# A streaming average pool: the last 14 of 64 row blocks loaded in pieces that step down in size, the small sizes in buffers of their own

## The chip, the cores and the metric

The kernel runs on one core of a Trainium2 chip. The metric is the device time of one execution in microseconds (us). All executions below are of the undisturbed ("fast") state, at a granted clock of 1.0. The span of the profile is 1.8 us shorter than that time (343.0 against 344.8 us in the profiled run of the kernel before).

Three engines matter. The DMA engines bring the input in and take the output out. VectorE (DVE in the profile) sums. ScalarE (ACT) multiplies by 1/16 and issues stores. SyncE (SP) only issues loads, and GpSimd (POOL) is idle before the change. A DMA that has landed raises a counter, its completion semaphore, and whoever needs its data waits for that counter. L75 in a view is line 75 of the kernel.

## The reference

```python
batch, channels, length = 32, 256, 4096      # float32, 134 MB
output_size = 256
for i in range(output_size):
    start = int(i * length / output_size)    # always 16 columns
    end = int((i + 1) * length / output_size)
    result[:, :, i] = np.mean(x[:, :, start:end], axis=-1)
```

The input is 8192 rows of 4096 numbers, 64 row blocks of 128 rows (2 MB each). Each block gives a 128 x 256 output (128 KB).

## The kernel before

The rows stream through. 31 pieces are pairs of blocks (4 MB, each partition one run of 32 KB), then there is one block of 2 MB, then the last block in four quarters of 512 KB. All 36 pieces rotate through the same four 32 KB-per-partition buffers.

```python
RBULK, IN_BUFS, TAIL_BLOCKS, TAIL_SPLITS = 2, 4, 2, 4       # (read from the environment; cut)
# pieces: (first block, blocks, first column, columns); pairs, one single, four quarters
# ... (cut)
sbuf = ctx.enter_context(tc.tile_pool(name="sbuf", bufs=IN_BUFS))
spool = ctx.enter_context(tc.tile_pool(name="spool", bufs=3))
opool = ctx.enter_context(tc.tile_pool(name="opool", bufs=3))

for (rb, nrb, c0, ncols) in pieces:
    # ... xin, oin: views of input and output (cut)
    xt = sbuf.tile([P, RBULK, length], x.dtype, name="xt")
    st = spool.tile([P, RBULK, length // k], mybir.dt.float32, name="st")
    ot = opool.tile([P, RBULK, length // k], out.dtype, name="ot")
    xv = xt[:, :nrb, :ncols]
    nc.sync.dma_start(out=xv, in_=xin)
    sv = st[:, :nrb, :nout]
    nc.vector.reduce_sum(out=sv, in_=xv.rearrange("p r (o k) -> p r o k", k=k),
                         axis=mybir.AxisListType.X)
    ov = ot[:, :nrb, :nout]
    nc.scalar.mul(out=ov, in_=sv, mul=inv_k)
    nc.scalar.dma_start(out=oin, in_=ov)
```

## Time and profile before

| | before |
|---|---|
| time, median of the first 5 runs | 344.8 us (344.77 to 345.09) |
| span | 343.0 us |
| bytes moved | 134.2 MB read, 8.4 MB written |
| VectorE busy | 278.2 us, 81% |
| DMA share and rate, 40 to 320 us | 1.00 to 1.01, 430 to 433 GB/s |

The first view is the table of windows of the kernel before. Its columns are the stretch, its length, the busy time of VectorE, ScalarE and GpSimd (with the number of instructions), the clock, the mean busy share of the 16 DMA engines, and GB/s. A packet's bytes and its time are counted in the stretch in which it starts, so a share can pass 1.

```profile
280.00:320.00 40.00, 34.25 (x4) 1.89 (x3) 0.00 (x0) 1.00 1.01 433
320.00:325.00 5.00, 3.35 (x2) 0.63 (x1) 0.00 (x0) 1.00 0.93 394
325.00:330.00 5.00, 5.00 (x1) 0.00 (x0) 0.00 (x0) 1.00 0.87 356
330.00:335.00 5.00, 5.00 (x2) 0.63 (x1) 0.00 (x0) 1.00 0.54 156
335.00:340.00 5.00, 4.38 (x5) 1.19 (x4) 0.00 (x0) 1.00 0.48 146
340.00:343.00 3.00, 0.38 (x1) 0.26 (x1) 0.00 (x0) 1.00 0.10 22
```

From 40 to 320 us the DMA engines are full. The Trainium skill ("DMA: Bandwidth & Descriptors", section "Where 436 GB/s comes from") puts the ceiling of the 16 ports at 435.2 GB/s; the 430 to 433 GB/s of this trace agree. From 320 us on the DMA share falls, to 0.54 in 330 to 335 us, while VectorE works without a break from 322.1 to 338.5 us. The last 23 us moved about 5.3 MB, 12.3 us of work at 432 GB/s, so some 10.7 us are lost here.

The second view is the end of the chain that ended last: start, duration, and what it was.

```profile
311.81 8.70 DVE st L75
...
320.52 9.79 DMA xt<-in_x_dram
...
330.74 4.42 DVE st L75
...
335.18 3.89 DMA xt<-in_x_dram
...
339.16 1.23 DVE st L75
...
340.41 0.26 ACT ot L81
```

Two of the quarters stand in this chain as loads, and each starts as a reduce ends: the second at 320.52, when the reduce of a pair gave up a buffer, and the fourth at 335.18, when the reduce of the 2 MB block did.

The third view is the groups of instructions by shape: line, engine, operation, output and input, count, busy time, mean of one in ns, and idle time before them.

```profile
L75 DVE TENSOR_REDUCE st<-xt 128x512 f32<-128x8192 f32 x31 | 269.3, 8686 | 61.6 <-DMA xt<-in_x_dram 61.6
L75 DVE TENSOR_REDUCE st<-xt 128x64 f32<-128x1024 f32 x4 | 4.7, 1213 | 0.6 <-DMA xt<-in_x_dram 0.6
L75 DVE TENSOR_REDUCE st<-xt 128x256 f32<-128x4096 f32 x1 | 4.4, 4409 | 0.0
```

A pair takes VectorE 8.69 us and arrives every 10.3 us. VectorE is therefore less than 20% faster than the stream.

### The profile page before, as it was taken

What the parts mean: (1) busy time and instruction counts of PE and PEld (TensorE: products, weight loads), DVE (VectorE), ACT (ScalarE), POOL (GpSimd) and SP (SyncE); (2) the same over time, 40 slices, a digit from 0 to 9 for tenths busy, and PEclk for the clock granted to TensorE, in tenths of its full rate; (3) what the DMA queues carried; (4) which work ended last, traced back from release to release, by engine and by line L of the source; (5) the groups of instructions that cost most, each with busy time, mean ns of one, the idle gap of its engine ahead of it and who ended that gap; (6) DMA issues with size and microseconds to landing.
All of it is one profiled execution on the core that took longest, in us unless ns stands there. A gap on an engine that the chain in (4) does not pass through costs nothing.

```text
span 343.0 us, 294 instructions
## 1 busy us (share of the span) xinstructions
DVE 278.2 (81%) x36; ACT 22.2 (6%) x37; POOL 0.2 (0%) x4
## 2 busy tenths in 40 slices
DVE  0488898888898888998888988888988888988896
ACT  1000000000000000000000000000000000000001
POOL 0000000000000000000000000000000000000000
DMA  8999999999999999999999999999999999999963
GB/s 321 447 436 413 451 427 418 451 412 440 447 406 442 447 401 455 430 411 455 427 421 451 409 436 451 406 447 431 410 454 431 413 458 411 430 451 415 425 239 107
DMA packets 10370, 142.63 MB, mean 416 GB/s; under 512 B 1664, under 2 KB 1792, under 8 KB 6272
## 3 DMA queue, kind: packets, MB, share of 16 engines
q1 hardware_dynamic: 5184, 134.22, 91.3%
q10 hardware_dynamic: 5184, 8.39, 6.4%
q14 instruction: 2, 0.02, 0.0%
HBM read 134.22 MB, written 8.39 MB: 416 GB/s over the span
## 4 chain that ended last, share of the span: by engine, by line
DMA 77%; DVE 22%; issue 0%; SPq 0%; ACT 0%; DVEq 0%
DMA xt<-in_x_dram 77%; DVE st L75 22%; SPq L73 0%; ACT ot L81 0%; DVEq L75 0%
## 5 line engine op out<-in xcount | busy, mean ns | idle before, releaser
L75 DVE TENSOR_REDUCE st<-xt 128x512 f32<-128x8192 f32 (+2 forms) x36 | 278.2, 7737 | 62.2 <-DMA xt<-in_x_dram 62.2
L81 ACT ACTIVATE ot<-st 128x512 f32<-128x512 f32 (+2 forms) x36 | 20.9, 582 | 317.7 <-DVE st L75 315.9
L81 ACT ACT_TABLE_LOAD x1 | 1.3, 1283 | 0.7 <-PEq L99 0.7
L99 POOL MEMSET const-uint8-127<- 128x1 uint8 x1 | 0.1, 103 | 0.0
L99 POOL MEMSET const-bfloat16-1.0<- 128x1 bf16 x1 | 0.1, 102 | 0.0
L99 POOL MEMSET const-float32-0.0<- 128x1 f32 x1 | 0.1, 99 | 0.2 <-issue 0.2
L99 POOL MEMSET const-float32-1.0<- 128x1 f32 x1 | 0.1, 99 | 0.0
## 6 DMA issues: line engine op xcount, KB each, us to landing
xt<-in_x_dram SPq DMA_DIRECT2D x31, 4096.0 KB, 32.5
out_dram<-ot ACTq DMA_DIRECT2D x31, 256.0 KB, 14.8
xt<-in_x_dram SPq DMA_DIRECT2D x1, 2048.0 KB, 27.6
xt<-in_x_dram SPq DMA_DIRECT2D x4, 512.0 KB, 6.9
out_dram<-ot ACTq DMA_DIRECT2D x1, 128.0 KB, 3.8
out_dram<-ot ACTq DMA_DIRECT2D x4, 32.0 KB, 1.8
```

The source lines that it names most:

```text
L75: nc.vector.reduce_sum(out=sv, in_=xv.rearrange("p r (o k) -> p r o k", k=k), axis=mybir.AxisListType.X,)
L81: nc.scalar.mul(out=ov, in_=sv, mul=inv_k)
L99: nc = _bacc.Bacc("TRN2", target_bir_lowering=False, num_devices=1)
```

## The change

The intent is to keep the DMA engines full to the last byte and to leave little work after it. The last 14 blocks are no longer pairs: ten are loaded as 2 MB pieces (still in the four big buffers), two in halves (1 MB), one in quarters (512 KB) and one in eighths (256 KB). Each of the three small sizes has as many buffers as its loads, so these 16 loads wait for no reduce to free a buffer. (Five of them still wait for the store of an earlier block, whose completion semaphore they take over: 17.8 us in all by SyncE's waits after.) The outputs of the blocks in halves and quarters are stored whole by GpSimd, that of the last block by ScalarE.

```diff
-    IN_BUFS = 4; TAIL_BLOCKS = 2; TAIL_SPLITS = 4          (from the environment; shortened)
+    # (shortened; the pools of sums and outputs are cut)
+    A_BUFS = 4; N1 = 10; NH = 2; NQ = 1; NE = 1; C_BUFS = 4; D_BUFS = 4
+    pa = tile_pool(bufs=A_BUFS)    # pairs and the ten single blocks
+    pc = tile_pool(bufs=C_BUFS)    # halves
+    pd = tile_pool(bufs=D_BUFS)    # quarters
+    pe = tile_pool(bufs=8)         # eighths
 ... (pairs as before; then N1 times the same with one block)
+    def tail_block(row0, splits, pool, tile_cols, last=False):
+        ob = ot.tile([P, output_size], f32, name="ob")
+        for (c0, ncols) in splits:
+            ...
+            xt = pool.tile([P, tile_cols], x.dtype, name="xc")
+            sv = st.tile([P, tile_cols // k], f32, name="sc")
+            xv = xt[:, :ncols]
+            nc.sync.dma_start(out=xv, in_=in_view(row0, 1, c0, ncols)[:, 0, :])
+            nc.vector.reduce_sum(out=sv[:, :nout], in_=xv.rearrange(...), ...)
+            nc.scalar.mul(out=ob[:, o0 : o0 + nout], in_=sv[:, :nout], mul=inv_k)
+        (nc.scalar if last else nc.gpsimd).dma_start(out=out_view(row0, 1, 0, output_size)[:, 0, :], in_=ob)
+    for _ in range(NH): tail_block(row0, [(0, half), (half, half)], pc, half)
+    for _ in range(NQ): tail_block(row0, [(i * quar, quar) for i in range(4)], pd, quar)
+    for _ in range(NE): tail_block(row0, [(i * eigh, eigh) for i in range(8)], pe, eigh, last=True)
```

More of the change, by code (lines that the diff above doesn't have):

```diff
@@ L33 @@
     n_blocks = n_rows // P
+    f32 = mybir.dt.float32
     RBULK = int(os.environ.get("AAP_RBULK", "2"))
-    IN_BUFS = int(os.environ.get("AAP_IN_BUFS", "4"))
-    TAIL_BLOCKS = int(os.environ.get("AAP_TAIL_BLOCKS", "2"))
-    TAIL_SPLITS = int(os.environ.get("AAP_TAIL_SPLITS", "4"))
-    pieces = []
-    nb_bulk = n_blocks - TAIL_BLOCKS
-    b = 0
-    while b < nb_bulk:
-        r = min(RBULK, nb_bulk - b)
-        pieces.append((b, r, 0, length))
-        b += r
-    while b < n_blocks - 1:
-        pieces.append((b, 1, 0, length))
-        b += 1
@@ L50 @@
-    if b < n_blocks:
-        assert length % (TAIL_SPLITS * k) == 0
-        c = length // TAIL_SPLITS
-        for s in range(TAIL_SPLITS):
-            pieces.append((b, 1, s * c, c))
-    sbuf = ctx.enter_context(tc.tile_pool(name="sbuf", bufs=IN_BUFS))
-    spool = ctx.enter_context(tc.tile_pool(name="spool", bufs=3))
-    opool = ctx.enter_context(tc.tile_pool(name="opool", bufs=3))
-    for (rb, nrb, c0, ncols) in pieces:
-        nout = ncols // k
-        row0 = rb * P
-        xin = x_flat[row0 : row0 + nrb * P, c0 : c0 + ncols]
-        xin = xin.rearrange("(p r) l -> p r l", r=nrb)
-        oin = out_flat[row0 : row0 + nrb * P, c0 // k : c0 // k + nout]
-        oin = oin.rearrange("(p r) l -> p r l", r=nrb)
-        xt = sbuf.tile([P, RBULK, length], x.dtype, name="xt")
-        st = spool.tile([P, RBULK, length // k], mybir.dt.float32, name="st")
-        ot = opool.tile([P, RBULK, length // k], out.dtype, name="ot")
-        xv = xt[:, :nrb, :ncols]
-        nc.sync.dma_start(out=xv, in_=xin)
-        sv = st[:, :nrb, :nout]
+    A_BUFS = int(os.environ.get("AAP_A_BUFS", "4"))
@@ new lines @@
+    N1 = int(os.environ.get("AAP_N1", "10"))
+    NH = int(os.environ.get("AAP_NH", "2"))
+    NQ = int(os.environ.get("AAP_NQ", "1"))
+    NE = int(os.environ.get("AAP_NE", "1"))
+    C_BUFS = int(os.environ.get("AAP_C_BUFS", "4"))
+    D_BUFS = int(os.environ.get("AAP_D_BUFS", "4"))
+    tail_blocks = N1 + NH + NQ + NE
+    nb_bulk = n_blocks - tail_blocks
+    assert nb_bulk >= 0 and nb_bulk % RBULK == 0
+    pa = ctx.enter_context(tc.tile_pool(name="pa", bufs=A_BUFS))
+    pc = ctx.enter_context(tc.tile_pool(name="pc", bufs=C_BUFS))
@@ new lines, with in_view @@
+    pd = ctx.enter_context(tc.tile_pool(name="pd", bufs=D_BUFS))
+    pe = ctx.enter_context(tc.tile_pool(name="pe", bufs=8))
+    sa = ctx.enter_context(tc.tile_pool(name="sa", bufs=2))
+    oa = ctx.enter_context(tc.tile_pool(name="oa", bufs=3))
+    st = ctx.enter_context(tc.tile_pool(name="st", bufs=4))
+    ot = ctx.enter_context(tc.tile_pool(name="ot", bufs=3))
+    half = length // 2
+    quar = length // 4
+    eigh = length // 8
+    def in_view(row0, nrb, c0, ncols):
+        v = x_flat[row0 : row0 + nrb * P, c0 : c0 + ncols]
+        return v.rearrange("(p r) l -> p r l", r=nrb)
@@ new lines, in out_view @@
+    def out_view(row0, nrb, o0, nout):
+        v = out_flat[row0 : row0 + nrb * P, o0 : o0 + nout]
+        return v.rearrange("(p r) l -> p r l", r=nrb)
+    blk = 0
+    while blk < nb_bulk:
+        nrb = RBULK
+        row0 = blk * P
+        xt = pa.tile([P, RBULK, length], x.dtype, name="xt")
+        sv = sa.tile([P, RBULK, output_size], f32, name="sv")
+        ov = oa.tile([P, RBULK, output_size], out.dtype, name="ov")
+        xv = xt[:, :nrb, :]
+        nc.sync.dma_start(out=xv, in_=in_view(row0, nrb, 0, length))
@@ L75 @@
         nc.vector.reduce_sum(
-            out=sv,
+            out=sv[:, :nrb, :],
             in_=xv.rearrange("p r (o k) -> p r o k", k=k),
@@ L79 @@
         )
-        ov = ot[:, :nrb, :nout]
-        nc.scalar.mul(out=ov, in_=sv, mul=inv_k)
-        nc.scalar.dma_start(out=oin, in_=ov)
+        nc.scalar.mul(out=ov[:, :nrb, :], in_=sv[:, :nrb, :], mul=inv_k)
+        nc.scalar.dma_start(out=out_view(row0, nrb, 0, output_size), in_=ov[:, :nrb, :])
+        blk += nrb
+    for _ in range(N1):
+        row0 = blk * P
+        xt = pa.tile([P, RBULK, length], x.dtype, name="xt")
+        sv = sa.tile([P, RBULK, output_size], f32, name="sv")
+        ov = oa.tile([P, RBULK, output_size], out.dtype, name="ov")
+        xv = xt[:, :1, :]
+        nc.sync.dma_start(out=xv, in_=in_view(row0, 1, 0, length))
+        nc.vector.reduce_sum(
+            out=sv[:, :1, :],
+            in_=xv.rearrange("p r (o k) -> p r o k", k=k),
+            axis=mybir.AxisListType.X,
+        )
+        nc.scalar.mul(out=ov[:, :1, :], in_=sv[:, :1, :], mul=inv_k)
+        nc.scalar.dma_start(out=out_view(row0, 1, 0, output_size), in_=ov[:, :1, :])
+        blk += 1
+    def tail_block(row0, splits, pool, tile_cols, last=False):
+        ob = ot.tile([P, output_size], f32, name="ob")
+        for (c0, ncols) in splits:
+            nout = ncols // k
+            o0 = c0 // k
+            xt = pool.tile([P, tile_cols], x.dtype, name="xc")
+            sv = st.tile([P, tile_cols // k], f32, name="sc")
+            xv = xt[:, :ncols]
+            nc.sync.dma_start(out=xv, in_=in_view(row0, 1, c0, ncols)[:, 0, :])
+            nc.vector.reduce_sum(
+                out=sv[:, :nout],
+                in_=xv.rearrange("p (o k) -> p o k", k=k),
+                axis=mybir.AxisListType.X,
+            )
+            nc.scalar.mul(out=ob[:, o0 : o0 + nout], in_=sv[:, :nout], mul=inv_k)
+        (nc.scalar if last else nc.gpsimd).dma_start(out=out_view(row0, 1, 0, output_size)[:, 0, :], in_=ob)
+    for _ in range(NH):
+        row0 = blk * P
+        tail_block(row0, [(0, half), (half, half)], pc, half)
+        blk += 1
+    for _ in range(NQ):
+        row0 = blk * P
+        tail_block(row0, [(i * quar, quar) for i in range(4)], pd, quar)
+        blk += 1
+    for _ in range(NE):
+        row0 = blk * P
+        tail_block(row0, [(i * eigh, eigh) for i in range(8)], pe, eigh, last=True)
+        blk += 1
+    assert blk == n_blocks
 _INS = ['x', 'output_size']
```

## The prediction

> **What bounds it now.** The input stream. In the windows view the DMA share is 1.00 to 1.01 and 430 to 433 GB/s in every 40 us stretch from 40 to 320 us; the Trainium skill ("DMA: Bandwidth & Descriptors", "Where 436 GB/s comes from") gives a ceiling of 435.2 GB/s, and this trace agrees. DVE is not the limit there: a bulk reduce takes 8.69 us (groups by form) against 10.3 us between pieces (timeline: reduces start at 280.85, 291.16, 301.49, 311.81) and waits 1.6 us for data each time.
>
> Only the ends are not full. Start: the first reduce begins at 13.06 us; the change leaves this alone. Tail: from 320 us to the end the windows view sums to about 5.3 MB, 12.3 us of work at 432 GB/s, and took 23 us: about 10.7 us lost. Reason (chain of waits): the last pieces rotate through the same four buffers. The last quarter, issued at 335.18, had waited for the reduce of the 2 MB piece (issued fourth before it), and landed 3.89 us later. The DMA idles near 330 and 334 us while DVE works off 8.7 + 4.4 us; then reduce 1.23, scale 0.26, and 2.3 us from the store's issue to the end.
>
> **What the change does.** The last 14 row blocks become ten 2 MB pieces, then 1 MB, 512 KB and 256 KB pieces with buffers of their own (8 MB, 16 loads), which no reduce has to free. The instruction order shows 8 completion semaphores shared round-robin by loads and stores, so each tail load waits for the eighth DMA before it; the worst, the third 256 KB load, waits for the store of the last 2 MB block. I estimate it is issued some 5 us before the queue could run dry. So the DMA stays full to the last input byte.
>
> **Cost.** From the trace's packet records: 32 KB 1213 ns, 16 KB 611, 4 KB 159, 2 KB 84, 1 KB 46, about 8 ns each beyond the bytes; 8 KB, about 310, is an estimate from these. Smaller rows add about 1.5 us of packet time (333.2 to 334.7 us per engine). The skill ("Bandwidth", "Measured") gives a 1 MB transfer alone 78% efficiency; here 512 KB pieces queued back to back moved 427 GB/s (327 to 329 us), so I do not charge that.
>
> Bulk landings come every 10.30 us from 13.06 us, so piece 25 of 25 lands at 260.3 us. The rest: 49.0 (ten 2 MB) + 9.9 + 5.1 + 5.4 (tail loads) + 6.2 (stores, same engines) = 75.6 us, times 0.993 (measured overlap) = 75.1: the last input lands at about 335.4 us. DVE at 4.41 us per 2 MB against 4.9 keeps up; by 148 ns + 1.04 ns per element (fit of 4409 and 1213 ns) a 512-element reduce is an estimated 0.68 us against 0.61 of DMA: backlog 0.2 to 0.5 us. Then 0.68 + 0.25 + store 2.3: span about 339, plus the 1.8 us between span and time: **340.8 us**, range **339.4 to 343.0**.
> Chances: faster by over 2% 0.03, within 2% 0.95, slower 0.02.
>
> **Signs.** DMA share about 1.0 until about 335 us; no DVE wait above 1 us in the tail; chain ending in a short reduce, one scale, one store; the ten-block stage still near 430 GB/s.
>
> **What would break it.** 2 KB rows running below the packet fit; semaphore sharing letting the queue run dry (1 to 3 us); GpSimd-issued stores landing late and holding the last block's scale, which waits for the first of them; a DVE backlog over the 16 small pieces.

## The result

| | before | after |
|---|---|---|
| time, median | 344.81 us (13 runs, 344.63 to 345.09) | 340.44 us (7 runs, 340.20 to 340.67) |
| span of the profiled run | 343.0 us | 338.9 us |
| last input landed (profile time) | 339.07 us | 335.17 us |
| mean rate over the span | 416 GB/s | 421 GB/s |

The ratio is 0.9873, with a 95% interval of 0.9862 to 0.9883. It is the mean time of one kernel's fast runs over that of the other's of the same rounds, so not quite the ratio of the medians. The change saves 1.3%. Outputs were correct.

The table of windows after (columns as above):

```profile
270.00:310.00 40.00, 35.68 (x9) 3.33 (x8) 0.00 (x0) 1.00 1.01 428
310.00:320.00 10.00, 9.22 (x4) 0.89 (x3) 0.00 (x0) 1.00 1.01 418
320.00:325.00 5.00, 5.00 (x3) 0.87 (x3) 0.68 (x1) 1.00 1.01 415
325.00:330.00 5.00, 5.00 (x5) 0.92 (x4) 0.54 (x1) 1.00 1.03 410
330.00:335.00 5.00, 5.00 (x8) 1.79 (x8) 0.54 (x1) 1.00 0.83 315
335.00:338.90 3.90, 0.95 (x2) 0.46 (x2) 0.00 (x0) 1.00 0.10 34
```

The DMA share now stays at about 1.0 until close to 334 us, when the input's packets begin to run out (the 0.83 of 330 to 335 us is the mean of both; the last landing is recorded at 335.17 us). The rate sags to 410 GB/s because smaller rows carry more packets: by the packet records a 4 KB packet takes 159 ns, which is 412 GB/s on 16 engines, where a 32 KB packet of 1213 ns gives 432. The groups of the 16 small reduces after, and what VectorE waited for in the whole run (from the waits: total us, times, longest):

```profile
L113 DVE TENSOR_REDUCE sc<-xc 128x128 f32<-128x2048 f32 x4 | 8.9, 2275 | 0.0
L113 DVE TENSOR_REDUCE sc<-xc 128x32 f32<-128x512 f32 x8 | 5.0, 680 | 0.0
L113 DVE TENSOR_REDUCE sc<-xc 128x64 f32<-128x1024 f32 x4 | 4.6, 1208 | 0.0
```

```profile
DVE sv L79 <- DMA xt<-in_x_dram: 51.6, 25, 12.9
DVE sv L95 <- DMA xt<-in_x_dram: 5.1, 6, 1.2
```

VectorE does not idle before any of the 16 small reduces (third column 0.0), and yet it is not late at the end. The last load lands at 335.17 us by the trace's landing records, and the timeline shows the last reduce starting 0.09 us later. That is no lag: in the kernel before, every reduce for which VectorE had waited idle, but for the first ones, also started 0.09 to 0.10 us after its load's landing.

```profile
335.27 0.69 DVE L113 TENSOR_REDUCE sc<-xc 128x32 f32<-128x512 f32 x1
...
335.99 0.23 ACT L118 ACTIVATE ob<-sc 128x32 f32<-128x32 f32 x1 [0.41 <-DVE sc L113]
336.25 0.34 ACTq L119 DMA_DIRECT2D out_dram<-ob  x1
```

So two streams, loads and reduces, finish together. The experiments ask which part of the change makes that so.

### The profile page after: what moved, and what is told of

Read it like the earlier page. It is cut to its first block, busy times and chain, and to the rows that moved or that the text cites. A ratio compares the mean times of both kernels' runs of the same rounds, so it can differ in the third digit from the quotient of the medians.

```text
span 338.9 us, 356 instructions
## 1 busy us (share of the span) xinstructions
DVE 279.2 (82%) x51; ACT 25.3 (7%) x52; POOL 2.0 (1%) x7
## 4 chain that ended last, share of the span: by engine, by line
DMA 70%; DVE 26%; issue 3%; ACT 0%; DVEq 0%
DMA xt<-in_x_dram 70%; DVE sv L79 17%; DVE sv L95 4%; DVE sc L113 4%; ACT ob L118 0%; DVEq L79 0%; DVEq L95 0%
## 5 line engine op out<-in xcount | busy, mean ns | idle before, releaser
L79 DVE TENSOR_REDUCE sv<-xt 128x512 f32<-128x8192 f32 x25 | 217.1, 8686 | 51.6 <-DMA xt<-in_x_dram 51.6
L95 DVE TENSOR_REDUCE sv<-xt 128x256 f32<-128x4096 f32 x10 | 43.9, 4415 | 5.1 <-DMA xt<-in_x_dram 5.1
L84 ACT ACTIVATE ov<-sv 128x512 f32<-128x512 f32 x25 | 15.7, 629 | 251.7 <-DVE sv L79 251.7
L113 DVE TENSOR_REDUCE sc<-xc 128x32 f32<-128x512 f32 (+2 forms) x16 | 18.3, 1211 | 0.0
L100 ACT ACTIVATE ov<-sv 128x256 f32<-128x256 f32 x10 | 4.2, 416 | 44.5 <-DVE sv L95 44.5
L118 ACT ACTIVATE ob<-sc 128x32 f32<-128x32 f32 (+2 forms) x16 | 4.1, 256 | 14.0 <-DVE sc L113 14.0
L119 POOL DMA_DIRECT2D out_dram<-ob x3 | 1.8, 587 | 329.9 <-ACT ob L118 329.9
```

What stands on the lines that cost most here:

```text
L79: nc.vector.reduce_sum(out=sv[:, :nrb, :], in_=xv.rearrange("p r (o k) -> p r o k", k=k), axis=mybir.AxisListType.X,)
L84: nc.scalar.mul(out=ov[:, :nrb, :], in_=sv[:, :nrb, :], mul=inv_k)
L95: nc.vector.reduce_sum(out=sv[:, :1, :], in_=xv.rearrange("p r (o k) -> p r o k", k=k), axis=mybir.AxisListType.X,)
L100: nc.scalar.mul(out=ov[:, :1, :], in_=sv[:, :1, :], mul=inv_k)
L113: nc.vector.reduce_sum(out=sv[:, :nout], in_=xv.rearrange("p (o k) -> p o k", k=k), axis=mybir.AxisListType.X,)
L118: nc.scalar.mul(out=ob[:, o0 : o0 + nout], in_=sv[:, :nout], mul=inv_k)
```

## The experiments

Theory 1 says that both halves of the change are needed: VectorE must have almost nothing left when the last bytes land (piece sizes), and the tail's loads must not wait for reduces (own buffers). Theory 2 says that only the buffer wait mattered. Theory 3 says that only the sizes mattered. "Before" and "after" below are the two kernels compared; every run gave a correct result.

| run | median us | ratio to before (95%) |
|---|---|---|
| own_buffers_old_sizes | 344.51 | 0.9989 (0.9974 to 1.0004) |
| shared_buffers_new_sizes | 345.13 | 1.0008 (0.9992 to 1.0025) |
| singles_shared | 342.58 | 0.9933 (0.9918 to 0.9948) |
| no_singles | 343.90 | 0.9971 (0.9956 to 0.9985) |
| four_singles | 340.44 | 0.9871 (0.9856 to 0.9885) |
| stores_on_scalar | 341.23 | 0.9894 (0.9879 to 0.9909) |
| coarse_end | 341.58 | 0.9903 (0.9889 to 0.9918) |
| singles_own_quarters | 342.53 | 0.9930 (0.9913 to 0.9946) |
| after_again | 340.51 | 0.9874 (0.9857 to 0.9890) |
| four_split_store | 340.33 | 0.9867 (0.9853 to 0.9882) |

The kernel before measured 344.87 to 344.95 us (medians) beside these runs.

### own_buffers_old_sizes: the buffer wait alone taken away

```diff
 (kernel before)
+    one = tile_pool(bufs=1); quart = tile_pool(bufs=4)
-        xt = sbuf.tile([P, RBULK, length], ...)
+        if ncols < length: xt = quart.tile([P, 1, ncols], ...)
+        elif nrb == 1:     xt = one.tile([P, 1, length], ...)
+        else:              xt = sbuf.tile([P, RBULK, length], ...)
```

> The kernel before with its old piece sizes, but the last 2 MB piece and the four 512 KB quarters have buffers of their own. Theory 1 (both parts are needed: VectorE must have little left to do when the last bytes land, and the tail loads must not wait for reduces): the loads now land by about 330 us, but VectorE still has 8.7 + 4.4 + 4 x 1.15 us to do from 322.1 us, so it ends near 339.5 instead of 340.4: 343.9 us, within 0.4; the tail shows no wait of VectorE. Theory 2 (buffer rotation alone is what the change cures): nearly the whole gain, 340.5 to 341.5 us.

Measured: 344.51 us, 0.2 us above the expected band, and only 0.4 us below before. The timeline of VectorE in this run:

```profile
322.20 8.69 DVE L82 TENSOR_REDUCE st<-xt 128x512 f32<-128x8192 f32 x1 [1.64 <-DMA xt<-in_x_dram]
330.81 4.41 DVE L82 TENSOR_REDUCE st<-xo 128x256 f32<-128x4096 f32 x1
335.13 4.59 DVE L82 TENSOR_REDUCE st<-xq 128x64 f32<-128x1024 f32 x4
```

The loads are no longer late: from the windows, 223 GB/s in 330 to 335 us against 156 before, and the landing records put the last input at 333.4 us, 5.7 us earlier than before. (The expectation said about 330, which was too early: the 4 MB after the landing of the last pair at 322.1 us need nearly 10 us.) But VectorE works without a break from 322.20 to 339.72. From first to last these are 17.5 us of reduces after the last pair has landed, while only 4 MB, less than 10 us of DMA, come after it. Theory 2 falls. (The interval of the ratio reaches 1.0004, so by it the 0.4 us is not clear of noise, though the four runs, 344.48 to 344.65, lie below all seven of the kernel before beside them, 344.81 to 345.11.) In the kernel before the late loads sat in the shadow of a late VectorE, and taking them away left VectorE's own lateness standing.

### shared_buffers_new_sizes: the sizes alone

```diff
 (kernel after, in tail_block)
-            xt = pool.tile([P, tile_cols], x.dtype, name="xc")
+            xt = pa.tile([P, RBULK, length], x.dtype, name="xt")
```

> The changed kernel with all its new piece sizes, but the 16 tail loads rotate through the four shared buffers. Theory 1: a load waits for the reduce four pieces earlier, four 256 KB pieces take 2.4 us of DMA, about the issue-to-landing time of one load, so the stream runs dry in the last two blocks: 1.5 to 3 us lost, 342 to 343.5 us, with VectorE waiting for loads in the tail. Theory 3 (the sizes alone give the gain): 340.4 us, within 0.4.

Measured: 345.13 us, the same as before within the interval and worse than expected: all of the gain is gone. First the loads of this run, then those of the kernel after (KB of one load, and the median from its issue to its landing), then VectorE's waits in this run and, from 315 us on, SyncE's longest:

```profile
xt<-in_x_dram SPq DMA_DIRECT2D x4, 512.0 KB, 4.9
xt<-in_x_dram SPq DMA_DIRECT2D x8, 256.0 KB, 3.6
```

```profile
xc<-in_x_dram SPq DMA_DIRECT2D x4, 512.0 KB, 10.0
xc<-in_x_dram SPq DMA_DIRECT2D x8, 256.0 KB, 7.3
```

```profile
DVE sc L113 <- DMA xt<-in_x_dram: 3.4, 5, 1.3
DVE sc L113 <- ACT ob L118: 0.4, 1, 0.4
```

```profile
SPq L112 <- DVE sc L113: 12.3, 12, 1.8
SPq L112 <- DVE sv L95: 3.1, 1, 3.1
```

The last view is the wait that the theory speaks of: 13 times a load could not be issued before a reduce had freed its buffer. A shorter time to landing is not good news here. In the kernel after a load spends 7.3 us from issue to landing because it stands in line behind others, and the line keeps the DMA engines fed. With shared buffers four 256 KB loads are all that can be under way. One takes about 3.6 us, and its bytes only about 0.7 us (8 packets of 84 ns on each engine), so the engines run dry (windows: 221 GB/s in 330 to 335 us). I had reckoned with 2.4 us from issue to landing, and so expected a loss of at most 3 us. Theory 3 falls too. The two halves do not add up: 0.4 us for the buffers, nothing for the full set of sizes, 4.4 us for both. (A milder set of sizes does gain in shared buffers, as the next run shows.)

### singles_shared and singles_own_quarters: half of the way

```diff
 singles_shared (kernel before):        -TAIL_BLOCKS = 2    +TAIL_BLOCKS = 12
 singles_own_quarters (kernel after):   -N1, NH, NQ, NE = 10, 2, 1, 1    +N1, NH, NQ, NE = 11, 0, 1, 0
                                        (the block in quarters stored whole by ScalarE)
```

> The kernel before with one number changed: 52 instead of 62 row blocks in pairs, then eleven 2 MB pieces and the four quarters, all in the four shared buffers. Theory 1: VectorE catches up in the 2 MB pieces, but the last quarter still waits for the reduce of the last 2 MB piece and lands some 7 us after that piece: about half of the gain, 342 to 343.2 us. Theory 2: no gain, 344.5 or more. Theory 3: most of the gain, 341 or less.

> The changed kernel with eleven 2 MB pieces and then only the four quarters, in buffers of their own: the run with eleven 2 MB pieces in shared buffers (342.58 us), cured of the buffer wait alone. Theory 1: VectorE still has the reduce of the last 2 MB piece (4.42) and four quarters (4.6) to do after that piece lands at about 328.5: it ends at 337.5 instead of 338.2, so 342.0 us, within 0.4: the sizes must step down. Rival (with own buffers two sizes are enough): 340.8 or less.

Measured: 342.58 and 342.53 us. The first is as expected: one changed number gives about half of the gain, since a piece of 2 MB leaves VectorE at most 4.4 us behind where a pair leaves it 8.7. The second adds own buffers for the quarters and beats the first by no more than the noise (expected 342.0, within 0.4, so 0.1 us outside). Its VectorE timeline:

```profile
328.65 4.42 DVE L95 TENSOR_REDUCE sv<-xt 128x256 f32<-128x4096 f32 x1 [0.78 <-DMA xt<-in_x_dram]
332.99 4.59 DVE L113 TENSOR_REDUCE sc<-xc 128x64 f32<-128x1024 f32 x4
```

The last reduce ends at 337.58 us against 338.20 in the first run, 0.6 us earlier, as the expectation said. The end of the span gives it back: the last store is now 128 KB instead of 32 KB and landed 1.70 us after its issue instead of 1.46, and from that landing to the end of the span 1.31 us passed instead of 0.87. What matters for the theory is that VectorE runs 8.9 us without a break after the last big piece, so with own buffers alone two sizes are not enough: the sizes must step down.

### no_singles and four_singles: how many 2 MB pieces

```diff
 (kernel after)   -N1 = 10    +N1 = 0     (no_singles)
 (kernel after)   -N1 = 10    +N1 = 4     (four_singles)
```

> The changed kernel without the ten 2 MB pieces (60 blocks in pairs, then the 16 tail loads in buffers of their own). Theory 1: after the last pair lands VectorE has 8.6 + 18.3 = 26.9 us to do and the DMA 22.8 plus 0.8 us of last reduce: VectorE ends 3.3 us late, less some 0.7 us of packets saved: 343.0 us, within 0.7; VectorE has no idle time in the tail. Theory 2 (own buffers are enough): 340 us or less.

> The changed kernel with four 2 MB pieces instead of ten. Theory 1 (VectorE's lag behind the loads must be worked off before the last bytes land): each 2 MB piece gives it about 0.8 us; by 26.95 + 4.33 N us of reduces against 23.6 + 5.24 N us of loads after the last pair, four pieces are just enough and three pairs of 2 MB pieces fewer save 0.4 us of packets: 340.6 us, within 0.5. A rival that needs all ten: 342 or more.

Measured: 343.90 and 340.44 us. In the run without 2 MB pieces VectorE never waits after the last pair, and its timeline shows 26.7 us of reduces from 311.76 to 338.47, where the expectation said 26.9:

```profile
311.76 8.69 DVE L79 TENSOR_REDUCE sv<-xt 128x512 f32<-128x8192 f32 x1 [1.64 <-DMA xt<-in_x_dram]
320.36 18.11 DVE L113 TENSOR_REDUCE sc<-xc 128x128 f32<-128x2048 f32 x16
```

The time is 0.2 us outside the expected band. After the last store had landed, 1.53 us passed to the end of the span, against 0.95 in the kernel after. The trace's instruction records show SyncE waiting at the end for the completion semaphores of all DMAs, two at a time and in a fixed order; the last store's semaphore stood in the fourth wait from the end here and in the second from it in the kernel after, and between the last two of these waits lies a gap of 0.44 us that the kernel after does not have. singles_own_quarters has the same gap in the same place, which is most of the 0.44 us that its end took longer than that of singles_shared. Why there is a gap is open.

Four 2 MB pieces are as good as ten. The balance "26.95 + 4.33 N us of reduces against 23.6 + 5.24 N us of loads", worked out from the trace of the kernel after, has its break-even at N = 3.7, and the runs at 0, 4 and 10 lie as it says. No run with one, two or three was made, so the break-even itself is not shown.

### coarse_end: halves to the end

```diff
 (kernel after)   -NH, NQ, NE = 2, 1, 1    +NH, NQ, NE = 4, 0, 0    (the last block stored by ScalarE, as in after)
```

> The changed kernel with its last two row blocks cut in halves (eight 1 MB loads, six buffers' worth replaced by the four of that size) instead of quarters and eighths. Theory 1: VectorE ends with a 2.28 us reduce instead of 0.68 after the last byte, which lands 0.6 us earlier for fewer small packets: about 341.4 us, within 0.5. Rival (the fine end does not matter): 340.4 or less.

Measured: 341.58 us, as expected. Now VectorE waits for loads again in the tail, and the last reduce alone lasts 2.29 us:

```profile
329.29 2.29 DVE L113 TENSOR_REDUCE sc<-xc 128x128 f32<-128x2048 f32 x1 [0.67 <-DMA xc<-in_x_dram]
332.06 4.68 DVE L113 TENSOR_REDUCE sc<-xc 128x128 f32<-128x2048 f32 x2 [0.48 <-DMA xc<-in_x_dram]
```

The fine end is worth 1.1 us by the medians: what remains after the last byte is the reduce of the last piece, 1.6 us longer here, while the last input landed 0.8 us earlier (334.36 us).

### stores_on_scalar: no stores from GpSimd

```diff
 (kernel after)
-        (nc.scalar if last else nc.gpsimd).dma_start(...)
+        nc.scalar.dma_start(...)
```

> The changed kernel with the three GpSimd-issued stores issued by ScalarE. Theory 1: stores are off the path: 340.4 us, within 0.6 (the last store lands on another completion semaphore, which may cost up to 0.6 at the end). Rival (the GpSimd queue is part of the gain): 341.5 us or more.

Measured: 341.23 us, 0.8 us above the kernel after (340.44) and 0.2 us above the band. It lies between the theory and its rival, and the waits tell why. First SyncE's waits from 315 us on in this run, then the same of the kernel after:

```profile
SPq L112 <- DMA out_dram<-ov: 7.2, 3, 2.8
SPq L112 <- DMA out_dram<-ob: 4.4, 2, 2.7
SPq L112 <- DMA xc<-in_x_dram: 0.9, 1, 0.9
```

```profile
SPq L112 <- DMA out_dram<-ov: 6.7, 3, 2.8
SPq L112 <- DMA xc<-in_x_dram: 3.2, 4, 1.2
```

In these programs loads from SyncE and stores from ScalarE take the same eight completion semaphores in turn (numbers 99, 100 and 103 to 108 in the records), and a load waits for the landing of the DMA that had its semaphore eight places earlier. With the three stores on ScalarE two of the tail's loads wait for a tail store (out_dram<-ob, 4.4 us), which itself waits for reduces. The sixth 256 KB load, for one, was issued at 331.21 us, when the store before it on its semaphore had landed at 331.20, and only 1.9 us before the fifth load landed; in the kernel after no tail load had less than 4.9 us of earlier loads ahead of it. After the fifth 256 KB load had landed the next one took 1.59 us to land instead of the 0.65 of the fifth (landing records), and VectorE stood still for it:

```profile
334.75 2.12 DVE L113 TENSOR_REDUCE sc<-xc 128x32 f32<-128x512 f32 x3 [0.88 <-DMA xc<-in_x_dram]
```

In the kernel after the three stores from GpSimd use three other semaphores (109 to 111), so no load waits for them. The last store of this run was issued 0.92 us later than in the kernel after (337.17 against 336.25), which is the whole difference. So the stores on GpSimd are part of the gain, though not for their speed. The prediction had named this wait as a danger, without saying that GpSimd was what kept it away.

### after_again and four_split_store: can it be bettered?

```diff
 (kernel after)
-    N1 = 10
+    N1 = 4
+            if last and o0 + nout == cut:        # cut: 192 of 256 columns
+                nc.gpsimd.dma_start(out=<columns 0 to cut>, in_=ob[:, :cut])
-        (nc.scalar if last else nc.gpsimd).dma_start(out=<all columns>, in_=ob)
+        if last: nc.scalar.dma_start(out=<columns from cut>, in_=ob[:, cut:])
+        else:    nc.gpsimd.dma_start(out=<all columns>, in_=ob)
```

> The changed kernel unaltered, as the yardstick for the next run on the same chip: 340.4 us, within 0.3.

> Four 2 MB pieces as in the earlier run, and the last row block stored in two parts: columns 0 to 191 from GpSimd as soon as their scales are done, the last 64 from ScalarE. A 32 KB store landed 1.46 us after issue where the 128 KB one took 1.70, so the end comes 0.24 us earlier; with the 0.35 us earlier end of the last reduce that four 2 MB pieces showed: 0.3 to 0.6 us below the changed kernel, about 340.0 us. Rival (the end of the span does not follow the last store): same as the changed kernel within 0.1.

Measured on the same chip: 340.51 us (340.46 to 340.66) and 340.33 us (340.19 to 340.43), four runs each. The difference of 0.18 us is smaller than expected. The last store did land 1.46 us after its issue instead of 1.70, but 0.2 us were given back between that landing and the end (1.16 us against 0.95), and the last reduce ended only 0.13 us earlier in this pair of traces. The runs of the two do not overlap, but this is 0.05%, which I would not build on. The kernel after is within a few tenths of what this scheme gives.

## Why the prediction was right

It said 340.8 us with a range of 339.4 to 343.0, and 340.44 came out; the span was to be about 339 us and was 338.9. Point by point:

- The stream as the bound: right. Moving 14 blocks to other sizes left the full stretches at 428 to 432 GB/s.
- The packet cost of smaller rows: right. Estimated 8 KB at 310 ns and taken as 84 for 2 KB; the packet records after have 309 and 85.4 ns (loads). I charged 1.5 us per engine. The records show 335.3 us after against 335.1 before; of the latter about 1.2 us are 4 KB packets that ran slowly in the broken stream (196 ns in the mean instead of 159), so like against like the cost was about 1.3 us.
- The last landing: 335.4 us predicted, 335.17 measured.
- VectorE's backlog at the end: 0.2 to 0.5 us predicted, none measured, and the reasoning was wrong here. The prediction set a reduce of 0.68 us against 0.61 us of DMA, so that VectorE would fall behind. Reduces of 512 elements do last 0.68 us, but they follow each other every 0.6 us, because the end of one overlaps the start of the next, and the last loads land every 0.65 us (the prediction's own 5.4 us for the eight loads are 0.68 each). So VectorE catches up: it starts 0.63 us after the landing of the first 256 KB load, 0.12 us after the fourth, and 0.09 us, as if it had been idle, after each of the last four. The error was small, since the term was.
- The drain: 0.68 + 0.25 + 2.3 us predicted, 0.69 + 0.23 + 2.65 measured (336.25 to 338.9). A 128 KB store lasts a little longer than the 32 KB one from which 2.3 us was read (1.70 against 1.5 us to landing). This term was too small by 0.35 us, while the landing and the backlog were put 0.2 and 0.2 to 0.5 us too late. That the span came out within 0.1 us of 339 is therefore in part luck.
- The reason given for the loss was wrong in its weight. The prediction said the last pieces lose time because they "rotate through the same four buffers". Taking away just that gained 0.4 us of 4.4. It also mentioned that VectorE "works off 8.7 + 4.4 us", and that was the larger part: 17.5 us of reduces after the last pair. The sum was right nevertheless, because it took both streams of the changed kernel into account rather than subtracting a wait from the old one.
- The signs: the DMA share was at 1.0 until the loads ran out near 334 us, 40 us with most of the ten 2 MB pieces ran at 428 GB/s, and the chain ends in reduce, scale and store. "No DVE wait above 1 us in the tail" holds for the 16 small pieces (no wait at all); in the ten 2 MB pieces two waits of about 1.2 us occurred, which cost nothing because the DMA was full.
- The dangers: semaphore sharing did not strike, although five of the 16 loads did wait for a store: each load was issued at least 4.9 us before the load ahead of it had landed. stores_on_scalar, with 1.9 us, shows how near it was. The late GpSimd stores did no harm: the first landed at 327.96 us, and the scale that had to wait for it ran at 331.62.

The reading that is argued and not shown: that the remaining distance to the stream's own time (about 330 us at 432 GB/s) is only the start, the slower small packets, the drain and the launch. No run here shortened the start.

## What to carry to other kernels

When a stream of loads feeds an engine that is only a little faster than the stream, look at what that engine still has to do when the last big piece lands: its lag is the time of one piece, and it shrinks only by the small difference of the rates, so let the pieces step down early enough (a balance of two lines told four pieces from none). Then make sure that the small loads can all be issued ahead, for which they need buffers of their own and must not share a completion semaphore with a store that comes late because it waits for the engine. Here buffers alone bought 0.4 us of 4.4, the fine sizes alone nothing, and the coarse step to 2 MB pieces alone 2.3; when a single cure gains nothing, try the pair before dropping it.

## What the Trainium skill lacked or had wrong

- "DMA: Bandwidth & Descriptors", sections "Measured" and "Rules for kernel authors": the table gives a 1 MB transfer 341 GB/s, 78%, and the rule asks for at least 1 MiB per DMA. The table is for transfers issued from GpSimd and does not tell how several loads in a queue fare; the page has a rate for a stream of 1 MiB loads elsewhere, but none was found for smaller loads in a queue. Here a queue of 512 KB and then 256 KB loads moved 410 GB/s, stores included (325 to 330 us after), and the 256 KB ones, 2 KB per row, landed every 0.70 us in the mean (329.60 to 335.17 us for eight), about 375 GB/s beside the stores.
- Same page, section "Rules for kernel authors": it says that spreading DMAs over SP, ACT and GpSimd does not help bandwidth and only saves issue time. Moving three 128 KB stores from ScalarE to GpSimd saved 0.8 us here, because it took them out of the ring of eight completion semaphores that the loads wait for. The "only" is too strong for that. That loads and stores share such a ring in a program built like this one was found on no page.
- Same page, section "Anatomy of one DMA — SWDGE (gpsimd) path": the fit of 2.0 us plus bytes gives an estimate of 2.6 us for 256 KB. The loads of shared_buffers_new_sizes, issued from SyncE with at most four under way, took 3.6 us in the median. The fit is for the other path and for a DMA alone, so this limits its use rather than contradicting it.
- No page was found that tells of the wait at the end of a program for the completions in a fixed order: from the last store's landing to the end of the span 0.81 to 1.53 us passed, depending on the kernel.
